# Alternating the order of the hi and lo weight products from group to group

## The chip, the cores and the metric

The kernel runs on one core of a Trainium2 chip. The metric is the device time of one execution in microseconds (us). Before the change it was 2684.91 us, the median of three runs (2683.16 to 2685.52). A profiled execution is one more run, with the hardware profiler on.

## The reference

The program is the trunk of a decoder with two layers, for 256 tokens of width 2048, in f32. Cut to what matters here:

```python
for layer in range(2):                       # 0: Mamba-2 SSD mixer, 1: RG-LRU mixer
    h = h + mixer(rms_norm(h), in_proj, ..., out_proj)
    h = h + (silu(u @ w_gate) * (u @ w_up)) @ w_down       # u = rms_norm(h), FFN of 5632
    h = h + (sigmoid(rms_norm(h) @ ple_gate)) * (p @ ple_up)
out = rms_norm(h)
# SSD: z, xbc, dt = split(u @ in_proj); short convolution, silu, chunked scan over 64 heads, gated norm
# RG-LRU: gate, xr = split(u @ in_proj); short convolution, block gates, linear scan, gelu(gate) * state
```

Nearly all the arithmetic lies in products of the activations with weights that are read once from memory in f32. (The real gate of the FFN and the per-layer embedding have their own norms; their form plays no part below.)

## The kernel before

Every weight matrix is cut into panels of 512 output columns. `panel()` computes one: it takes four PSUM banks (of eight), one for each 128 columns, and adds up the products over all blocks k of 128 input rows. The precision of f32 is kept by splitting: an activation block x holds its rounded half and the rest side by side, 128 x 512; a weight block is split into a rounded part `hi` and a rest `lo`. A weight block goes into the sum by a product of hi with all of x (128 x 512, line 268) and a product of lo with the first half of x (128 x 256, line 265).

Weights come in tiles `raw` of two k by 512 columns (512 KB, a DMA from SyncE's queue, line 231; five buffers). ScalarE casts a raw tile to a hi tile (line 239), VectorE subtracts and leaves a lo tile (line 240); each has four buffers. One tile serves eight products (two k by four banks). `group()` takes up 16 products of each kind, that is two hi tiles and two lo tiles: first 16 hi products, then 16 lo products. In the last group of a panel the second half is sorted by bank, so that bank 0 is complete first. A panel with 16 k has four groups. The last panel of the program takes its last group in another way (`apart`); the change leaves that as it was.

Behind the products, `product()` counts and now and then advances two queues of other work: `post` (what follows a panel: totals of banks, convolutions, activations, gates) and `side` (the SSD scan). These put small instructions on VectorE and ScalarE and transposes on TensorE (lines 448 and 507: transposes of sp, cs and xs in the SSD part) between the products. The total of a bank is a copy by ScalarE (line 153) and an add by VectorE (line 156). The scheduler of the language orders the instructions of every engine at build time; each engine then runs its list strictly in that order, and waits where an operand isn't there. So when the products ask for their tiles in another order, the lists of all the engines come out different.

Names that the text below uses: `a_neg`, `sp_624`, `sp_625`, `dt_v`, `adt`, `cs` belong to the step sizes and their running sums in the SSD part, in the first panels (lines 364 to 452); `sums` is a table in DRAM made from cs by DMAs (line 105), from which the tiles `e` of the scan are read; `xs` are the SSD inputs behind their activation; `gt`, `th`, `xc` belong to the RG-LRU (lines 354 to 669).

Of the kernel before, what the change touches and what calls it, by code (L numbers as in the profile page):

```python
# [18 lines left out]
T = 256  # L19
# [25 lines left out]
class Trunk:  # L45
# [197 lines left out]
    def panel(self, w, xs, pump=1.4, kt=KG, nb=NB, pre=None, post=True, apart=False):  # L243

        nc = self.nc
        banks = [self.bank() for _ in range(nb)]
        nk = w.shape[0] * kt
        todo = []
        size = RUN // nb
        count = [0, 0]

        def product(j, k, part, lo):
            b, x, wt = banks[j], xs[k], part[lo][:, j * P:(j + 1) * P]
            if apart and j == nb - 1:  # L260
                for h in range(1 if lo else 2):
                    nc.tensor.matmul(b[:, :T], wt, x[:, h * T:(h + 1) * T], start=k + lo + h == 0,
                                     stop=lo == 1 and k == nk - 1, skip_group_check=True)
            elif lo:
                self.last_product = nc.tensor.matmul(b[:, T:], wt, x[:, :T], start=False, stop=k == nk - 1,  # L265
                                                     skip_group_check=True)
            else:
                self.last_product = nc.tensor.matmul(b, wt, x, start=k == 0, stop=False, skip_group_check=True)  # L268

            count[0] += 1 if lo else 2  # L270
            while count[0] >= 3 * nb * (count[1] + 1):
                count[1] += 1
                if post:
                    self.advance(self.post)
                self.pump(pump)

        def group(last):
            if last and apart:
                for j in range(nb):
                    for lo in (0, 1):  # L280
                        for k, part in todo:
                            product(j, k, part, lo)
            else:
                for k, part in todo:
                    for j in range(nb):
                        product(j, k, part, 0)
                order = [(j, k, part) for k, part in todo for j in range(nb)]
                if last:
                    order.sort(key=lambda o: o[0])
                for j, k, part in order:  # L290
                    product(j, k, part, 1)
            todo.clear()

        k = 0
        for g in range(w.shape[0]):
            for parts in self.weights(w[g], nb * P, kt, pre and (lambda: pre(g)), bool(pre) and g < 2):
                for part in parts:
                    todo.append((k, part))
                    k += 1
                    if k == nk or len(todo) == size and not (apart and k > nk - 2 * size):  # L300
                        group(k == nk)
        if post:
            self.drain_post()
        return banks
# [579 lines left out]
```

## Time and profile before

| | |
|---|---|
| median of three runs | 2684.91 us |
| profiled execution, its own time | 2682.07 us |
| its span in the trace | 2680.3 us |
| granted TensorE clock, mean | 0.996 |
| TensorE busy | 2648.2 us (99%) |
| VectorE busy | 1822.4 us (68%) |
| ScalarE busy | 1501.7 us (56%) |
| GpSimd busy | 32.5 us (1%) |

Busy time is the time in which an engine executes. Rows of a timeline give the start, the length, the engine, the source line, the operation, output and inputs, and the number of instructions of that form in a row; in brackets stands the idle time just before, and what ended it. Matmuls overlap, so a row of products ends after the next one begins; the distance between starts is what counts.

### The profile page before, as it was taken

What the parts mean: (1) busy time and instruction counts of PE and PEld (TensorE: products, weight loads), DVE (VectorE), ACT (ScalarE), POOL (GpSimd) and SP (SyncE); (2) the same over time, 40 slices, a digit from 0 to 9 for tenths busy, and PEclk for the clock granted to TensorE, in tenths of its full rate; (3) what the DMA queues carried; (4) which work ended last, traced back from release to release, by engine and by line L of the source; (5) the groups of instructions that cost most, each with busy time, mean ns of one, the idle gap of its engine ahead of it and who ended that gap; (6) DMA issues with size and microseconds to landing.
All of it is one profiled execution on the core that took longest, in us unless ns stands there. A gap on an engine that the chain in (4) does not pass through costs nothing.

```text
span 2680.3 us, 40689 instructions
## 1 busy us (share of the span) xinstructions
PE 2648.2 (99%) x15346; PEld 2334.0 (87%) x15346; DVE 1822.4 (68%) x3066; ACT 1501.7 (56%) x2399; POOL 32.5 (1%) x70
## 2 busy tenths in 40 slices
PE   9899999999999999999999999999999999999998
PEld 7788888888888888888888888888888888888887
DVE  7888878855566655555666899977666555665667
ACT  7677755544444444444455678856444444444555
POOL 0011100000000000000000000000000000000000
PEclk9999999999999999999999999999999999999999
DMA  6767655555555555555655565555555555556553
GB/s 232 244 209 219 190 181 184 186 189 189 184 193 189 189 182 190 195 190 189 194 187 188 172 195 176 196 189 189 189 189 189 196 190 180 189 193 202 186 187 125
DMA packets 141915, 510.77 MB, mean 191 GB/s; under 512 B 15901, under 2 KB 16349, under 8 KB 141661
## 3 DMA queue, kind: packets, MB, share of 16 engines
q1 hardware_dynamic: 141719, 508.18, 57.9%
q8 instruction: 120, 1.97, 0.3%
q14 instruction: 76, 0.62, 0.1%
HBM read 505.92 MB, written 5.05 MB: 191 GB/s over the span
## 4 chain that ended last, share of the span: by engine, by line
PE 90%; DVE 6%; ACT 2%; issue 1%; DMA 1%; SPq 0%; DVEq 0%; ACTq 0%
PE bank L268 58%; PE bank L265 30%; DVE c L356 1%; DVE lo L240 1%; ACT hi L239 1%; DVE t L156 1%; DMA raw<-in_w_ssd_in_dram 1%; PE bank L523 1%; DVE t L163 1%; DVE xc L356 0%; PE bank L625 0%; ACT L88 0%; PE bank L525 0%; PE bank L507 0%; ACT s L153 0%
## 5 line engine op out<-in xcount | busy, mean ns | idle before, releaser
L268 PE MATMUL bank<-x,hi 128*128 128x512 f32 x7360 | 1771.7, 392 | 12.0 <-ACT hi L239 9.9
L268 PEld LDWEIGHTS bank<-x,hi 128*128 128x128 f32 x7360 | 1351.6, 189 | 277.4 <-ACT hi L239 12.7
L239 ACT CAST hi<-raw 128x1024 fp32r<-128x1024 f32 (+1 forms) x932 | 972.1, 1048 | 1031.6 <-PE bank L268 962.6
L240 DVE TENSOR_TENSOR lo<-raw,hi 128x1024 fp32r<-128x1024 f32 (+1 forms) x932 | 1107.2, 1220 | 503.4 <-issue 431.1
L265 PEld LDWEIGHTS bank<-x,lo 128*128 128x128 f32 x7360 | 949.5, 191 | 42.0 <-DVE lo L240 4.8
L265 PE MATMUL bank<-x,lo 128*128 128x256 f32 x7360 | 967.2, 283 | 4.4 <-DVE lo L240 4.4
L156 DVE TENSOR_TENSOR t<-bank,s 128x256 f32<-128x256 f32 x448 | 161.9, 418 | 291.3 <-ACT s L153 290.5
L153 ACT COPY s<-bank 128x256 f32<-128x256 f32 x496 | 160.3, 374 | 13.4 <-PE bank L265 4.8
L163 DVE TENSOR_TENSOR t<-t,r 128x256 f32<-128x256 f32 x216 | 83.2, 427 | 0.0
L356 DVE SCALAR_TENSOR_TENSOR c<-t,vecs,c 128x255 f32<-128x255 f32 (+1 forms) x144 | 63.1, 487 | 0.1
L145 ACT ACTIVATE x<-h,vecs 128x256 fp32r<-128x256 f32 x96 | 47.4, 501 | 17.0 <-DVE h L337 13.8
L88 ACT ACT_TABLE_LOAD x43 | 55.2, 1283 | 1.1 <-DVE c L356 0.3
L337 DVE TENSOR_TENSOR h<-h,t 128x256 f32<-128x256 f32 x144 | 54.2, 420 | 0.2
L146 DVE SCALAR_TENSOR_TENSOR x<-h,vecs,x 128x256 fp32r<-128x256 f32 x96 | 45.5, 480 | 5.9 <-ACT x L145 5.9
L88 ACT ACTIVATE e<-e,ncs 128x256 f32<-128x256 f32 (+1 forms) x128 | 45.3, 442 | 0.1
L176 DVE TENSOR_TENSOR acc<-acc,q 128x256 f32<-128x256 f32 x104 | 43.8, 421 | 2.2 <-ACT q L169 1.4
L169 ACT ACTIVATE q<-h 128x256 f32<-128x256 f32 x104 | 41.4, 405 | 4.7 <-DVE h L337 3.8
L88 ACT ACTIVATE sg<-t 128x256 f32<-128x256 f32 x88 | 32.3, 412 | 18.7 <-DVE t L163 18.7
L137 ACT CAST x<-t 128x256 fp32r<-128x256 f32 x88 | 31.8, 403 | 18.8 <-DVE t L717 18.8
L488 DVE TENSOR_TENSOR e<-e,cm 128x768 f32<-128x768 f32 x32 | 31.0, 970 | 12.6 <-ACT e L88 6.5
L403 POOL TENSOR_SCALAR_AFFINE_SELECT e<-e 128x256 f32<-128x256 f32 x64 | 31.8, 519 | 274.1 <-DMA e<-sums 236.7
L138 DVE TENSOR_TENSOR x<-t,x 128x256 fp32r<-128x256 f32 x88 | 33.3, 421 | 0.0
(121 smaller groups left out, 679.1 us busy)
## 6 DMA issues: line engine op xcount, KB each, us to landing
raw<-in_w_ffn_in_dram SPq DMA_DIRECT2D x352, 512.0 KB, 4.6
raw<-in_w_ffn_out_dram SPq DMA_DIRECT2D x176, 512.0 KB, 4.4
raw<-in_w_ssd_in_dram SPq DMA_DIRECT2D x158, 512.0 KB, 4.5
raw<-in_w_ssd_out_dram SPq DMA_DIRECT2D x64, 512.0 KB, 4.3
raw<-in_w_ple_gate_dram SPq DMA_DIRECT2D x64, 512.0 KB, 4.3
raw<-in_w_lru_in_dram SPq DMA_DIRECT2D x64, 512.0 KB, 4.2
raw<-in_w_lru_out_dram SPq DMA_DIRECT2D x32, 512.0 KB, 4.7
e<-sums SPq DMA_DIRECT2D x32, 384.0 KB, 6.0
```

The costliest lines, as they stand in the source:

```text
L88: i = self.nc.scalar.activation(out, in_, func, **kw).ins
L145: nc.scalar.activation(x[:, :T], src, AF.Copy, scale=w)
L146: nc.vector.scalar_tensor_tensor(x[:, T:], src, w, x[:, :T].bitcast(F32), ALU.mult, ALU.subtract)
L153: nc.scalar.copy(s, b[:, T:])
L156: nc.vector.tensor_tensor(t, b[:, :T], s, ALU.add)
L163: self.nc.vector.tensor_tensor(t, t, r, ALU.mult)
L239: self.last_hi = nc.scalar.copy(hi, src).ins
L240: nc.vector.tensor_tensor(lo, src, hi.bitcast(F32), ALU.subtract)
L265: self.last_product = nc.tensor.matmul(b[:, T:], wt, x[:, :T], start=False, stop=k == nk - 1, skip_group_check=True)
L268: self.last_product = nc.tensor.matmul(b, wt, x, start=k == 0, stop=False, skip_group_check=True)
L337: self.nc.vector.tensor_tensor(hb, hb, t, ALU.add)
L356: nc.vector.scalar_tensor_tensor(out[:, d:], t[:, :T - d], self.vec(cw, (3 - d) * ntap + i), out[:, d:], ALU.mult, ALU.add)
```

## The change

Within a panel, groups of odd number (the second, the fourth) take their 16 lo products first and their 16 hi products behind them; groups of even number stay hi first. So at the boundary of an odd group the kind does not change: 32 lo products stand in a row, then 32 hi products. The last group's second half is sorted by bank as before, whichever kind it is, and the flag that ends a bank's sum goes to the last product.

```diff
-        def product(j, k, part, lo):
+        turn = [0]
+
+        def product(j, k, part, lo, stop):
...
-                self.last_product = nc.tensor.matmul(b, wt, x, start=k == 0, stop=False, skip_group_check=True)
+                self.last_product = nc.tensor.matmul(b, wt, x, start=k == 0, stop=stop, skip_group_check=True)
...
         def group(last):
+            end = lambda k: last and k == nk - 1
...
-                for k, part in todo:
-                    for j in range(nb):
-                        product(j, k, part, 0)
                 order = [(j, k, part) for k, part in todo for j in range(nb)]
+                for j, k, part in order:
+                    product(j, k, part, turn[0], False)
                 if last:
                     order.sort(key=lambda o: o[0])
+                turn[0] = 1 - turn[0]
                 for j, k, part in order:
-                    product(j, k, part, 1)
+                    product(j, k, part, turn[0], end(k))
```

The number of instructions stays the same on every engine that computes. Lines of helpers stand three lines lower in the changed file; the hi product is line 270 there, the lo product line 267. In TensorE's list a hi product is followed by a lo product 467 times before and 245 times now, a lo product by a hi product 439 times before and 245 times now.

Three places show how the lists change. First the start of the program, in the panels whose results feed the scan. TensorE before (the transposes of sp_625 and cs are line 448):

```order
L265 MATMUL bank<-x,lo 128x256 x16
L268 MATMUL bank<-x,hi 128x512 x16
L265 MATMUL bank<-x,lo 128x256 x16
L268 MATMUL bank<-x,hi 128x512 x9
L448 MATMUL bank<-ident,sp_625 128x128 x2
L268 MATMUL bank<-x,hi 128x512 x7
L265 MATMUL bank<-x,lo 128x256 x8
L448 MATMUL bank<-ident,cs 128x128 x2
```

And TensorE there now:

```order
L270 MATMUL bank<-x,hi 128x512 x32
L267 MATMUL bank<-x,lo 128x256 x32
L270 MATMUL bank<-x,hi 128x512 x3
L451 MATMUL bank<-ident,sp_625 128x128 x2
L270 MATMUL bank<-x,hi 128x512 x5
L451 MATMUL bank<-ident,cs 128x128
L270 MATMUL bank<-x,hi 128x512
L451 MATMUL bank<-ident,cs 128x128
L270 MATMUL bank<-x,hi 128x512 x23
```

The transposes of sp_625 moved from the tenth place of the next group's hi products to the fourth place of this group's, those of cs from that group's lo products to behind this group's eighth hi product.

VectorE at the same place, around the small instruction on a_neg, before:

```order
L435 TENSOR_SCALAR a_neg<-a_neg 128x1
L163 TENSOR_TENSOR t<-t,r 128x256
L370 TENSOR_TENSOR sp_623<-sp_623,sp_622 128x256
L356 SCALAR_TENSOR_TENSOR c<-t,vecs,c 128x255
L371 TENSOR_TENSOR sp_624<-sp_623 128x256
L356 SCALAR_TENSOR_TENSOR c<-t,vecs,c 128x254
```

VectorE there now:

```order
L163 TENSOR_TENSOR t<-t,r 128x256
L373 TENSOR_TENSOR sp_623<-sp_623,sp_622 128x256
L438 TENSOR_SCALAR a_neg<-a_neg 128x1
L240 TENSOR_TENSOR lo<-raw,hi 128x1024
L374 TENSOR_TENSOR sp_624<-sp_623 128x256
L359 SCALAR_TENSOR_TENSOR c<-t,vecs,c 128x255
```

The group's first lo tile moved from behind the work on c and sp_625 to directly behind a_neg; its second lo tile still follows that work.

Second, SyncE's queue a little later, where the table sums is made. Before:

```order
L231 DMA raw_1046<-in_w_ssd_in_dram 128x1024
L231 DMA raw_1052<-in_w_ssd_in_dram 128x1024
L105 DMA sums_97<-cs_692 64x384
L231 DMA raw_1104<-in_w_ssd_in_dram 128x1024
L231 DMA raw_1110<-in_w_ssd_in_dram 128x1024
L105 DMA sums_97<-sums_97 8x2x12288 x3
L105 DMA sums_97<-sums_97 5x2x12288
```

Now:

```order
L231 DMA raw_1046<-in_w_ssd_in_dram 128x1024
L105 DMA sums_97<-cs_700 64x384
L105 DMA sums_97<-sums_97 8x2x12288 x3
L105 DMA sums_97<-sums_97 5x2x12288
L231 DMA raw_1052<-in_w_ssd_in_dram 128x1024
L231 DMA raw_1104<-in_w_ssd_in_dram 128x1024
L231 DMA raw_1110<-in_w_ssd_in_dram 128x1024
```

Three weight loads moved behind all the DMAs of sums.

Third, ScalarE in the RG-LRU, around the gelu of gt. Before, with the names of the weight tiles:

```order
L239 CAST hi_16834<-raw_16832 128x1024
L88 ACT_TABLE_LOAD
L88 ACTIVATE th0_16652<-th0_16652 128x256 x2
L88 ACTIVATE th1_16653<-th1_16653 128x256 x2
L88 ACT_TABLE_LOAD
L88 ACTIVATE gt0_16148<-gt0_16148 128x256 x2
L88 ACTIVATE gt1_16149<-gt1_16149 128x256 x2
```

Now:

```order
L88 ACT_TABLE_LOAD
L88 ACTIVATE gt0_16148<-gt0_16148 128x256 x2
L88 ACTIVATE gt1_16149<-gt1_16149 128x256 x2
L153 COPY s_16810<-bank_16514 128x256
L153 COPY s_16814<-bank_16515 128x256
L153 COPY s_16818<-bank_16516 128x256
L239 CAST hi_16834<-raw_16832 128x1024
```

The cast of the tile from raw_16832 moved from ahead of both table loads to behind the gelu and three copies.

## Rows read from the trace of the kernel before

**Rows 1.** The page, busy time, share of the span and instructions of each engine

```profile
PE 2648.2 (99%) x15346; PEld 2334.0 (87%) x15346; DVE 1822.4 (68%) x3066; ACT 1501.7 (56%) x2399; POOL 32.5 (1%) x70
```

**Rows 2.** The page's costliest groups: busy, mean ns, idle time before and what ended it

```profile
L268 PE MATMUL bank<-x,hi 128*128 128x512 f32 x7360 | 1771.7, 392 | 12.0 <-ACT hi L239 9.9
L265 PE MATMUL bank<-x,lo 128*128 128x256 f32 x7360 | 967.2, 283 | 4.4 <-DVE lo L240 4.4
```

**Rows 3.** Timeline of TensorE in the program's last panel: start, length, line, operation

```profile
2654.24 2.00 PE L268 MATMUL bank<-x,hi 128*128 128x512 f32 x8
...
2662.62 0.64 PE L262 MATMUL bank<-x,hi 128*128 128x256 f32 x4
```

**Rows 4.** Timeline of TensorE in panels of the RG-LRU's output

```profile
1800.43 3.82 PE L268 MATMUL bank<-x,hi 128*128 128x512 f32 x16
...
1839.39 3.82 PE L268 MATMUL bank<-x,hi 128*128 128x512 f32 x16
```

**Rows 5.** Timeline of TensorE around the transposes of xs, third head group

```profile
206.38 0.49 PE L507 MATMUL bank<-ident,xs 128*128 128x128 f32 x3
207.22 0.33 PE L507 MATMUL bank<-ident,xs 128*128 128x128 f32 x1 [0.35 <-ACT xs L88]
207.30 3.00 PE L268 MATMUL bank<-x,hi 128*128 128x512 f32 x12
210.14 0.60 PE L507 MATMUL bank<-ident,xs 128*128 128x128 f32 x4
210.50 0.71 PE L268 MATMUL bank<-x,hi 128*128 128x512 f32 x2
```

**Rows 6.** Line 507, idle time of its queues until: us, times

```profile
  ACT xs L88: 6.0, 11
```

**Rows 7.** Timeline of TensorE at the program's start

```profile
64.45 3.82 PE L268 MATMUL bank<-x,hi 128*128 128x512 f32 x16
72.67 3.78 PE L265 MATMUL bank<-x,lo 128*128 128x256 f32 x16 [4.39 <-DVE lo L240]
76.24 2.64 PE L268 MATMUL bank<-x,hi 128*128 128x512 f32 x9
```

**Rows 8.** Stretch of TensorE: length, busy (products), granted clock, DMA share, GB/s

```profile
72.60:76.20 3.60, 3.54 (x16) 0.50 0.69 175
```

**Rows 9.** Timeline of VectorE in the same stretch

```profile
65.75 0.15 DVE L435 TENSOR_SCALAR a_neg<-a_neg 128x1 f32<-128x1 f32 x1 [0.95 <-ACT a_neg L88]
...
66.48 0.48 DVE L356 SCALAR_TENSOR_TENSOR c<-t,vecs,c 128x255 f32<-128x255 f32 x1
...
71.39 1.22 DVE L240 TENSOR_TENSOR lo<-raw,hi 128x1024 fp32r<-128x1024 f32 x1
...
76.67 0.42 DVE L380 TENSOR_TENSOR sp<-sp,sp 128x256 f32<-128x256 f32 x1
```

**Rows 10.** Timeline of ScalarE, a cast behind a weight load

```profile
76.20 1.05 ACT L239 CAST hi<-raw 128x1024 fp32r<-128x1024 f32 x1 [2.47 <-DMA raw<-in_w_ssd_in_dram]
```

**Rows 11.** Timeline of SyncE's DMA issues

```profile
84.54 2.86 SPq L105 DMA_DIRECT2D sums<-sums  x4
87.93 4.32 SPq L231 DMA_DIRECT2D raw<-in_w_ssd_in_dram  x2
```

**Rows 12.** Timeline of ScalarE, the cast of the first of these two loads

```profile
104.60 1.05 ACT L239 CAST hi<-raw 128x1024 fp32r<-128x1024 f32 x1 [4.34 <-DMA raw<-in_w_ssd_in_dram]
```

**Rows 13.** Timeline of ScalarE in the RG-LRU

```profile
1634.74 1.34 ACT L88 ACTIVATE gt<-gt 128x256 f32<-128x256 f32 x4
1635.98 0.90 ACT L153 COPY s<-bank 128x256 f32<-128x256 f32 x3
```

**Rows 14.** Timeline of TensorE in the RG-LRU

```profile
1636.03 3.96 PE L268 MATMUL bank<-x,hi 128*128 128x512 f32 x16
```

**Rows 15.** Timeline of VectorE behind an output panel

```profile
1420.83 2.35 DVE L240 TENSOR_TENSOR lo<-raw,hi 128x1024 fp32r<-128x1024 f32 x2
```

**Rows 16.** Timeline of TensorE there

```profile
1421.89 3.82 PE L268 MATMUL bank<-x,hi 128*128 128x512 f32 x16
```

## What the change is expected to do: the prediction

> **What bounds the kernel now.** I read the page's shares first. TensorE is busy for 2648.2 of 2680.3 us, VectorE and ScalarE much less [rows 1], so only what makes TensorE shorter, or makes it wait, counts. In the costliest groups the reader is to see the idle time in front of the products: 12.0 us before the hi products, 4.4 us before the lo products, over 7360 of each [rows 2]. The hi and lo tiles are thus nearly always there in time, and the question is whether they still are when another kind is asked for first. Then come the timelines: the spacing of starts tells what a switch of kind costs, and at four places the rows of VectorE, ScalarE and SyncE tell when a tile is made and when it would now be wanted.
>
> The sum is made against the profiled execution's own 2682.07 us, 1.8 us around its span of 2680.3; it lies 2.84 us under the median, 2684.91, so 2.84 is added at the end. A change under 0.2%, 5.4 us, counts here as no change: from 2679.5 to 2690.3.
>
> **Switches removed.** The last panel takes 8 hi and 8 lo products in turn: three periods from 2654.24 to 2662.62 [rows 3], 2.793 us each, so 16 + 16 products with two pairs of switches take 5.587. In groups of 16 + 16 seven periods run from 1800.43 to 1839.39 [rows 4], 5.566 each, with one pair. A pair of switches costs 0.021 us. By the counts in the section on the change, 222 switches from hi to lo and 194 from lo to hi go, 208 pairs: **-4.2 us**. No gain of another kind is in the products: their number and shapes stay, and both rows are full streams.
>
> The Trainium skill, in "TensorE: Matmul & The Clock Gate", section "Back-to-back issue gap", gives the distance of products that are taken singly as their columns at 2.4 GHz and 2.5 ns more, whatever stood before. By it regrouping is worth nothing, and the sum would be 4.2 us higher. The trace has a difference, though one of 0.02 us in 5.6.
>
> **Transposes of xs in the SSD part.** Behind the panels of a head group, four transposes wait for the last xs on ScalarE. The first four take from 206.38 to the next product at 207.30, 0.92 us with a wait of 0.35; the second four, with nothing to wait for, from 210.14 to 210.50, 0.36 [rows 5]. So 0.56 us per head group where it occurs; the line's queues waited 11 times, 6.0 us [rows 6], and that counts TensorE and its weight loads both, about five head groups. In the new order ScalarE makes xs earlier against the products, and the lo tiles wanted in its place are made in time by VectorE, so I take the whole: 5 x 0.56 = **-2.8 us** (from 0 to -3.0, half of the 6.0).
>
> **The program's start.** This is the largest loss. Before, the hi products of one group begin at 64.45, then TensorE waits 4.39 us for the first lo tile, the lo products begin at 72.67, and the next group's hi products at 76.24 [rows 7]. The 16 lo products in 72.60 to 76.20 run at half the clock: the granted clock there is 0.50, the level of 1.2 GHz, after the 4.39 us of idle time [rows 8].
>
> Now the lo products come first. The first lo tile stands directly behind a_neg, which ends at 65.90 [rows 9], and takes 1.22: it is there at 67.1, and eight products run. The second is still behind the work on c and sp that before filled 66.48 to 71.39 [rows 9], 4.9 us: 67.1 + 4.9 + 1.2 = 73.2. TensorE waits about five microseconds, and I assume the half clock after it for as long as before: 8 lo in 1.8 to 75.0, four hi in 1.8, twelve more at 0.23 (3.82 over 16, rows overlap, [rows 7]) in 2.7, end at 79.6 against 76.24, **+3.4**. Between these hi products now stand the transposes of sp and cs. That of sp is covered: sp was written at 76.67 to 77.09 [rows 9], now a little earlier, and TensorE is there at about 76.4. cs is not: VectorE makes it behind a lo tile whose hi cast, held by its load, ends at 77.25 [rows 10]; add 1.2 for that lo tile and about 1.4 for the scans (four small instructions, the size of those in [rows 9]), so 79.8, and TensorE is there at 78.2: **+1.6**. Together +5.0.
>
> Then SyncE: three weight loads now stand behind the DMAs of sums. The first two loads that stood behind them before were issued from 87.93, and sums from 84.54 [rows 11], and the first was there only at 104.60, when its cast began after 4.34 us of waiting [rows 12]: 16.7 us from issue to use. Now sums is issued some two microseconds earlier, since cs has fewer lo tiles before it on VectorE, and the first load behind it at about 85.7. By the same 16.7 it would be cast at 102.4 and its lo tile ready at 104.7 (1.05 and 1.22). It is wanted by the fourth group after this one, lo first, second tile: 76.24 + 5.0 + three groups of 5.566 + 0.6 for the transposes, about 98.5, and 0.96 for the first tile's eight products: 99.5. The loss is between 0, if the load overtakes the copies, and 5.2 and another 1.7 for the clock (16 products at half of it took 3.57, from 72.67 to 76.24, in place of 1.91). I take 2, nearer to nothing, since in the rows of before the queue also carried two loads ahead of sums. The start: **+7 us**, from +3.4 to +11.9.
>
> **RG-LRU.** ScalarE cast the first hi tile of the group at 1636.03 [rows 14] ahead of both table loads. Now it stands behind gt (1634.74 + 1.34) and three copies that end at 1636.8 [rows 13]: ready at 1637.8, **+1.8** (0 if the list before it has become shorter). The lo tiles of the next, lo first, group are wanted 3.65 us earlier, and VectorE has seven instructions of some 0.48 ahead of the second one, up to 3.4; later tiles of this stretch would be late too, but a wait there gives the others time. I take +2.2: **+4.0 us** in all, from 0 to +5.2.
>
> **Output panels.** Where totals and norms lie ahead of the lo tiles on VectorE, the order of these does not change. Two lo tiles take 1420.83 to 1423.18 [rows 15]; a group that begins at 1421.89 [rows 16] lo first wants the first at once and the second 0.96 later. The first is ready at 1422.05 (+0.16), the second at 1423.18 against 1423.01 (+0.17): 0.33 us. I count 14 such panels, from FFN, SSD and RG-LRU outputs: **+4.6 us** (from 0, if the totals too come earlier, since the sorted half is now the longer one). In the FFN's input panels, more than half of all groups, VectorE has time, and I cost the earlier lo tiles at nothing; if that cover were gone, each group would lose what the output panels lose.
>
> **The sum.** -4.2 - 2.8 + 7 + 4.0 + 4.6 = +8.6. 2682.07 + 8.6 + 2.84 = **2693.5 us**.
>
> **Rivals.** 1. *The new lists hide every loss* (faster). The scheduler knows when a lo tile is wanted and may have put each in time; the gain in switches and xs stays: -7.0, 2677.9 us. For it: idle time ahead of products is only 16 us now [rows 2], so tiles have time. Against it: the first lo tile moved, the second did not. 0.16.
>
> 2. *Only the start's own wait remains* (no change). The load behind sums overtakes it, and the RG-LRU and output panels absorb their lateness: -7.0 + 5.0 = -2.0, 2682.9 us. For it: the waits of a few tenths in the output panels are within the error of such a count. Against it: the order of ScalarE at gt. 0.24.
>
> 3. *A switch costs nothing*, the rest as forecast: 2697.7 us. Against it stand rows 3 and 4; for it that they differ by 0.02 us only, near the hundredth in which they are given. 0.08. This is what the Trainium skill's rule in "Back-to-back issue gap" would make of it.
>
> 4. *The loads behind sums hold up the start in full*, and the half clock follows: start +11.9, RG-LRU +5.2, outputs +4.6, gains -7.0: +14.7, 2699.6 us. For it: the one load that the rows show behind sums took 16.7 us. 0.15.
>
> **How the numbers follow.** The forecast has 0.37. It and rivals 1 to 4 make 1. The forecast's own range is 2688 to 2699; a seventh of it falls within no change. So faster 0.16, no change 0.24 + 0.05 = 0.29, slower 0.55. The range for 8 in 10 leaves out the lower half of rival 1 and the far end of rival 4: 2678 to 2703.
>
> **What would show it.** In the changed kernel's timeline of TensorE: a wait for a lo tile between eight and eight lo products near 68 to 73, a wait at the transposes of cs near 78 to 80, and one for a lo or hi tile near 99 to 105; waits for hi near 1636; idle time of tenths ahead of lo products behind output panels. In the page, line 267's idle time would rise from 4.4 to about 15 us, and the transposes' waits for xs vanish. It is wrong if switches turn out to be worth clearly more than 0.02 us a pair, if idle time ahead of lo products does not rise, or if SyncE's loads behind sums land within a few microseconds of their issue.

## The result, and the profile after

The changed kernel takes 2707.28 us (median of four runs, 2707.11 to 2707.64), the kernel before, in the same session, 2685.22. The ratio is 1.0083, 95% interval 1.0065 to 1.0100: 22 us slower. The forecast was slower, 2693.5 us, in a range up to 2703; the direction was right, but the forecast change, 8.6 us, is less than half of the measured one.

The page after, first the busy times, then the groups of the two products (columns as in [rows 2]):

```profile
span 2705.6 us, 40570 instructions
PE 2656.3 (98%) x15346; PEld 2342.8 (87%) x15346; DVE 1866.9 (69%) x3066; ACT 1502.5 (56%) x2399; POOL 42.9 (2%) x70
...
L270 PE MATMUL bank<-x,hi 128*128 128x512 f32 x7360 | 1737.7, 392 | 6.7 <-ACT hi L239 6.0
...
L267 PE MATMUL bank<-x,lo 128*128 128x256 f32 x7360 | 944.1, 285 | 29.9 <-DVE lo L240 29.6
```

Against [rows 1, 2] the reader is to see two things. The wait ahead of the lo products rose from 4.4 to 29.9 us, as the new order asks for lo first. And TensorE is busy 8.1 us longer (2648.2 to 2656.3) with the same products: some ran at the lower clock. (The two groups' own busy times fell, because the overlap of a hi with a lo product at a switch counts in both, and there are fewer switches.) The span grew by 25.3; what isn't busy, 17.2 us, is waiting. The profiled execution of the kernel before lies 3 us under its median, so differences between the traces are 3 us larger than the 22 of the medians.

Where the time goes is best seen from the start of the weight product that has n others before it in both traces (the RG-LRU's small gate products left out), and their difference. Products 0 to 2592 are the SSD's input panels, the first head panel from 544, the last eight panels, for the gate z, from 1568; its output panels end at 3616, the first FFN at 7904, the first embedding at 8416, the RG-LRU at 9952.

| product | start before | later after by |
|---|---|---|
| 128 | 30.4 | 3.1 |
| 384 | 82.7 | 6.5 |
| 512 | 105.7 | 13.8 |
| 640 | 129.4 | 17.9 |
| 704 | 146.3 | 15.3 |
| 1664 | 351.9 | 11.6 |
| 7680 | 1405.2 | 10.2 |
| 8704 | 1589.6 | 11.7 |
| 9216 | 1693.3 | 25.2 |
| 14080 | 2547.7 | 24.5 |
| last | 2665.4 | 25.4 |

The start costs 15.3 us: 3.1 in the first panel, 3.4 up to product 384, 7.4 up to 512, 1.4 up to 704. (The 17.9 at product 640 sets a product behind a wait against one that in the kernel before has its wait still ahead.) The SSD's head groups give 3.7 back, the panels up to 7680 a little more, and the RG-LRU costs 13.5.

**The start.** TensorE's timeline after, in the stretch of [rows 7], and, ahead of it, two waits in the first panel:

```profile
13.35 1.22 PE L267 MATMUL bank<-x,lo 128*128 128x256 f32 x8 [0.32 <-DVE lo L240]
16.08 2.08 PE L267 MATMUL bank<-x,lo 128*128 128x256 f32 x8 [1.51 <-DVE lo L240]
...
69.92 1.45 PE L267 MATMUL bank<-x,lo 128*128 128x256 f32 x8 [2.22 <-DVE lo L240]
76.30 2.08 PE L267 MATMUL bank<-x,lo 128*128 128x256 f32 x8 [4.93 <-DVE lo L240]
78.18 1.48 PE L270 MATMUL bank<-x,hi 128*128 128x512 f32 x3
79.46 0.63 PE L451 MATMUL bank<-ident,sp 128*128 128x128 f32 x2
79.74 1.96 PE L270 MATMUL bank<-x,hi 128*128 128x512 f32 x5
81.54 0.27 PE L451 MATMUL bank<-ident,cs 128*128 128x128 f32 x1
```

VectorE there, the rows that answer to [rows 9]:

```profile
68.58 0.15 DVE L438 TENSOR_SCALAR a_neg<-a_neg 128x1 f32<-128x1 f32 x1 [0.35 <-ACT a_neg L88]
68.65 1.22 DVE L240 TENSOR_TENSOR lo<-raw,hi 128x1024 fp32r<-128x1024 f32 x1
...
75.03 1.22 DVE L240 TENSOR_TENSOR lo<-raw,hi 128x1024 fp32r<-128x1024 f32 x1
```

The two lo tiles start 6.4 us apart, the second behind the work on c and sp, and TensorE waits 4.93 us between eight and eight lo products. The transposes of sp and cs (line 451) wait for nothing.

Next come two waits that the table shows at products 512 and 640. SyncE's issues, the cast of the first load behind sums, and TensorE:

```profile
85.64 2.86 SPq L105 DMA_DIRECT2D sums<-sums  x4
88.60 10.09 SPq L231 DMA_DIRECT2D raw<-in_w_ssd_in_dram  x5
```

```profile
104.90 1.04 ACT L239 CAST hi<-raw 128x1024 fp32r<-128x1024 f32 x1 [1.96 <-DMA raw<-in_w_ssd_in_dram]
...
144.80 3.88 ACT L239 CAST hi<-raw 128x1024 fp32r<-128x1024 f32 x4
```

```profile
107.25 2.07 PE L267 MATMUL bank<-x,lo 128*128 128x256 f32 x8 [5.87 <-DVE lo L240]
...
147.31 2.93 PE L267 MATMUL bank<-x,lo 128*128 128x256 f32 x12 [4.69 <-DVE lo L240]
```

The load issued at 88.60 is cast at 104.90, 16.3 us later; in the kernel before it was 16.7 [rows 11, 12]. The wait at 147.31 is of another kind: the four casts at 144.80 stand in ScalarE's list behind the exponentials of the first head group. The kernel before waits at the same place, for its hi tiles:

```profile
133.57 3.87 ACT L239 CAST hi<-raw 128x1024 fp32r<-128x1024 f32 x4
...
134.65 3.38 PE L268 MATMUL bank<-x,hi 128*128 128x512 f32 x8 [3.25 <-ACT hi L239]
```

So this wait is not new; lo first, TensorE waits there for a subtraction behind the cast too, and the net loss is 1.4 us (13.8 late at product 512, 15.3 at 704).

After these waits the products run slowly. Stretches of TensorE, columns as in [rows 8] (length, busy, granted clock):

```profile
16.00:20.00 4.00, 3.92 (x14) 0.57 1.04 412
...
76.00:80.00 4.00, 3.70 (x14) 0.50 0.51 136
107.20:111.00 3.80, 3.75 (x13) 0.50 0.80 256
147.00:151.00 4.00, 3.69 (x17) 0.50 0.63 181
1662.00:1666.00 4.00, 3.40 (x12) 0.50 0.51 151
```

0.50 is the level of 1.2 GHz. The kernel before has the stretch of [rows 8] and one more, behind its wait at 134.65.

**RG-LRU.** Three of TensorE's waits, and VectorE at the second of these:

```profile
1604.28 1.22 PE L267 MATMUL bank<-x,lo 128*128 128x256 f32 x8 [1.49 <-DVE lo L240]
...
1662.61 1.65 PE L267 MATMUL bank<-x,lo 128*128 128x256 f32 x6 [2.44 <-DVE lo L240]
...
1706.03 2.08 PE L267 MATMUL bank<-x,lo 128*128 128x256 f32 x8 [2.35 <-DVE lo L240]
```

```profile
1657.67 1.22 DVE L240 TENSOR_TENSOR lo<-raw,hi 128x1024 fp32r<-128x1024 f32 x1
1658.81 0.42 DVE L138 TENSOR_TENSOR x<-xc,x 128x256 fp32r<-128x256 f32 x1
1659.14 0.42 DVE L138 TENSOR_TENSOR x<-gt,x 128x256 fp32r<-128x256 f32 x1
...
1661.33 1.22 DVE L240 TENSOR_TENSOR lo<-raw,hi 128x1024 fp32r<-128x1024 f32 x1
```

Between the two tiles stand seven small instructions, VectorE is never idle, and TensorE waits 2.44 us. In all there are six waits for lo tiles in the RG-LRU, 9.6 us, and one for a hi tile, 0.56 us.

### The profile page after: what moved, and what is told of

It is laid out like the page before. It is cut to its first block, busy times and chain, and to the rows that moved or that the text cites. A ratio compares the mean times of both kernels' runs of the same rounds, so it can differ in the third digit from the quotient of the medians.

```text
span 2705.6 us, 40570 instructions
## 1 busy us (share of the span) xinstructions
PE 2656.3 (98%) x15346; PEld 2342.8 (87%) x15346; DVE 1866.9 (69%) x3066; ACT 1502.5 (56%) x2399; POOL 42.9 (2%) x70
## 4 chain that ended last, share of the span: by engine, by line
PE 89%; issue 6%; DVE 4%; ACT 1%; POOL 0%; DVEq 0%; POOLq 0%; ACTq 0%
PE bank L270 57%; PE bank L267 30%; DVE lo L240 1%; PE bank L526 1%; PE bank L628 0%; DVE t L156 0%; ACT hi L239 0%; DVE h L340 0%; DVE acc L176 0%; PE bank L528 0%; PE bank L510 0%; PE bank L630 0%; POOL e L406 0%; PE bank L187 0%; DVE xc L359 0%
## 5 line engine op out<-in xcount | busy, mean ns | idle before, releaser
L270 PE MATMUL bank<-x,hi 128*128 128x512 f32 x7360 | 1737.7, 392 | 6.7 <-ACT hi L239 6.0
L270 PEld LDWEIGHTS bank<-x,hi 128*128 128x128 f32 x7360 | 1367.4, 189 | 281.6 <-ACT hi L239 7.2
L240 DVE TENSOR_TENSOR lo<-raw,hi 128x1024 fp32r<-128x1024 f32 (+1 forms) x932 | 1119.3, 1221 | 589.1 <-ACT hi L239 368.3
L267 PEld LDWEIGHTS bank<-x,lo 128*128 128x128 f32 x7360 | 926.1, 192 | 56.5 <-DVE lo L240 34.2
L267 PE MATMUL bank<-x,lo 128*128 128x256 f32 x7360 | 944.1, 285 | 29.9 <-DVE lo L240 29.6
L153 ACT COPY s<-bank 128x256 f32<-128x256 f32 x496 | 178.5, 371 | 389.0 <-PE bank L270 373.9
L156 DVE TENSOR_TENSOR t<-bank,s 128x256 f32<-128x256 f32 x448 | 184.8, 421 | 167.6 <-ACT s L153 164.8
L359 DVE SCALAR_TENSOR_TENSOR c<-t,vecs,c 128x255 f32<-128x255 f32 (+2 forms) x144 | 65.5, 498 | 0.5 <-ACT c L357 0.4
L491 DVE TENSOR_TENSOR e<-e,cm 128x768 f32<-128x768 f32 x32 | 31.0, 968 | 19.4 <-issue 10.4
L720 DVE TENSOR_TENSOR t<-t,sg 128x256 f32<-128x256 f32 x88 | 37.2, 422 | 1.5
L714 DVE TENSOR_TENSOR sg<-sg,r 128x256 f32<-128x256 f32 x88 | 34.8, 420 | 0.7
```

The source lines that it names most:

```text
L153: nc.scalar.copy(s, b[:, T:])
L156: nc.vector.tensor_tensor(t, b[:, :T], s, ALU.add)
L240: nc.vector.tensor_tensor(lo, src, hi.bitcast(F32), ALU.subtract)
L359: nc.vector.scalar_tensor_tensor(out[:, d:], t[:, :T - d], self.vec(cw, (3 - d) * ntap + i), out[:, d:], ALU.mult, ALU.add)
```

## The experiments

Theory A: the loss is made at single places where a tile stands late in VectorE's or ScalarE's list or behind sums in the queue, made larger by the lower clock behind the wait. Theory B: every alternated group costs a little. Theory C: buffers and loads, not lists, make the tiles late. A list is the order of one engine's instructions. Ratios are to the kernel before, run on the same chip beside each set (medians 2682.9 to 2683.1).

**Parts of the program.** A flag chooses per panel whether the order alternates:

```diff
                 for j, k, part in order:
                     product(j, k, part, turn[0], end(k))
+                turn[0] = turn[0] if self.swap else 0
```

Only in the six first panels. Expected:

> Alternating only in the six first panels (the four B, C panels, dt, and the first head panel). Theory A, the loss is made at single places, where a lo tile asked for early stands late in VectorE's list, and the idle time there puts the TensorE clock to its lower level for some microseconds: the start alone costs +13 to +18 us on before, since the changed kernel is 17.9 us late after the sixth panel, and later waits for xs give a part back or not. Theory B, every alternated group costs a little, the same everywhere: six of about 120 panels cost no more than 2 us.

Measured: 2695.39 us, +12.4; ratio 1.0047 (1.0033 to 1.0061). That is a little under the range expected. (The profiled execution took 2698.20; in its trace the kernel is 15.9 us late at product 704 and 16.8 at 1664.)

Only in the RG-LRU's input panels and first four output panels. Expected:

> Alternating only in the RG-LRU's input panels and its first four output panels. Theory A: the changed kernel goes from 11.7 to 25.2 us late in this stretch, so alone it costs +11 to +14 us. Theory B (the same small cost in all groups): 12 of about 120 panels, +2 to +3 us.

Measured: 2699.77 us, +16.7; 1.0062 (1.0048 to 1.0076). That is above the range expected: in the trace 3.2 us are lost in the RG-LRU's first input panel, where the changed kernel loses nothing.

Everywhere else. Expected:

> Alternating everywhere but in these two stretches: the SSD's other panels, output panels, FFN, per-layer embedding. Theory A: what remains is the gain, -0.02 us for a pair of switches, some 180 pairs, and the waits for xs in the SSD part if these panels make them go: -4 to -7 us against before. Theory B: the loss stays, +15 to +20 us.

Measured: 2683.49 us, +0.4; 1.0001 (0.9992 to 1.0010).

Theory B falls: nearly the whole loss is in the first two parts. The gain expected of the rest did not come. Its trace has the waits for xs gone, but three small ones for lo in the head groups, between 160 and 360 us, in their place (us, times, longest):

```profile
PE bank L268 <- DVE lo L241: 1.0, 3, 0.4
```

At product 704 it is 1.5 us late, in panels that are unchanged (the kernel with the RG-LRU's order alone is 1.4 late there); the difference is 1.0 at product 5120, 0.6 at 7680, and 1.5 at the end, since the panels around the embedding take back what switches give. The three parts add up to +29.5 against +22.1. Two reasons can be seen in the traces: the head groups gave 3.7 us back only where they alternate behind a late start (0.9 lost with the start's order alone, 0.4 with the rest's), and the RG-LRU alone lost 3.2 in its first panel.

**Loads ahead of sums.** Six more steps of the side work ahead of the DMAs of sums:

```diff
             self.dts, self.ncs = dts, ncs
             yield
             yield
+            for _ in range(6):
+                yield
```

> The changed kernel with the DMAs of sums six steps later in the side work, so that the load of raw_1048 and the two behind it are issued ahead of most of sums, as before. If the wait of 5.87 us near 101 is the load behind the sums copies, it goes and with it the half clock behind it: -5 to -8 us against the changed kernel (+14 to +17 on before), unless tiles e come later and the first head group waits for them. If that wait comes from the order on VectorE or ScalarE alone, the time stays within 1 us of the changed kernel's +22.

Measured: 2698.59 us, ratio 1.0059 (1.0043 to 1.0074), +15.5, so 6.5 below the changed kernel, as expected. One load now goes ahead of the copies within sums, two between them:

```profile
88.00 0.33 SPq L231 DMA_DIRECT2D raw<-in_w_ssd_in_dram  x1
88.38 1.46 SPq L105 DMA_DIRECT2D sums<-sums  x2
89.94 1.05 SPq L231 DMA_DIRECT2D raw<-in_w_ssd_in_dram  x2
91.04 1.41 SPq L105 DMA_DIRECT2D sums<-sums  x2
```

TensorE at that place:

```profile
102.77 7.44 PE L270 MATMUL bank<-x,hi 128*128 128x512 f32 x32
110.05 2.07 PE L267 MATMUL bank<-x,lo 128*128 128x256 f32 x16
113.28 2.43 PE L267 MATMUL bank<-x,lo 128*128 128x256 f32 x16 [1.16 <-DVE lo L240]
```

The wait of 5.87 is gone; at product 512 the kernel is 7.6 us late, not 13.8. The load behind sums cost 6.2 us, wait and slow products together. Behind that place the two kernels differ in other ways too (5.2 against 15.3 us late at product 800, 4.9 against 11.6 at 1664), so that the 6.5 of the totals is not this wait alone.

**The place in the list.** The scheduler takes a priority for what it is given; here hi and lo tiles get one some instructions earlier, in the RG-LRU panels alone:

```diff
+            with self.tc.high_priority(self.lead):
                 self.last_hi = nc.scalar.copy(hi, src).ins
                 nc.vector.tensor_tensor(lo, src, hi.bitcast(F32), ALU.subtract)
```

> The changed kernel; only in the RG-LRU's input panels and first four output panels the casts and subtractions that make hi and lo tiles get a priority 80 instructions earlier in the scheduler, so they stand ahead of gates, scans and convolutions in ScalarE's and VectorE's lists. Products and buffers stay. Theory A (lo tiles are late by their place in VectorE's list): the waits for lo between 1595 and 1710 go, and the half clock behind them: the stretch costs some 0 to 5 us in place of 13.5, so -8 to -13 us against the changed kernel, +9 to +14 on before. Theory C (tiles are late because their four buffers come free too late, or their loads land too late): no list can help, the time stays at +22 on before within 2 us.

Measured: 2697.9 us, +15.0; 1.0054 (1.0039 to 1.0069), 7 below the changed kernel, 1 short of the range expected. Waits between 1590 and 1710, changed kernel and this one (us, times, longest):

```profile
PE bank L267 <- DVE lo L240: 9.6, 6, 2.4
PE bank L270 <- ACT hi L239: 0.6, 1, 0.6
```

```profile
PE bank L269 <- DVE lo L242: 3.1, 4, 0.9
PE bank L272 <- DVE t L157: 1.2, 1, 1.2
...
```

Products and buffers are the same, and most of the wait went; the stretch from product 8704 to 9216 costs 5.9 us, not 13.5. Theory C falls for the RG-LRU: most of its loss is one of lists. It did not go wholly: waits for lo of 3.1 us remain, and one for t, the total of a bank, is new.

The same in all panels, by 80 and by 160 instructions, and in the kernel before:

> The changed kernel with that priority in all panels. Theory A: the losses at the start shrink too, where they come from lists (first lo tiles, the five microseconds near 71, the load behind sums, since sums moves in SyncE's queue): -10 to -20 us against the changed kernel, +2 to +12 on before; side work that now comes later may cost some of it. Theory C: at the start loads and buffers decide, and no more than 3 us are won there.

> As before, 160 instructions earlier. Theory A: as with 80, or a little better in the RG-LRU; if side work becomes late, totals hold up banks and the time is longer than with 80 by some microseconds. Theory C: no difference to the changed kernel.

> The kernel before with the same priority of 80, as a control: if the priority is worth something of itself (the waits of 9.9 and 4.4 us for hi and lo tiles in before), -2 to -8 us; if only the new order needs it, within 2 us of before.

Measured: 2711.73 (1.0107, 1.0090 to 1.0124), 2718.29 (1.0129, 1.0114 to 1.0144) and 2712.40 us (1.0108, 1.0092 to 1.0123). All three expectations missed in the total; only the guess that 160 might take some microseconds longer than 80 came true. The traces say why. At product 1664 the changed kernel with 80 is 1.1 us late and with 160 1.6 us early, against 11.6 without: the whole loss of the start, against the kernel before, can be taken away by lists. In the RG-LRU 80 lowers the loss to 4.4 us, but 160 leaves 11.8: waits for t have taken the place of those for lo. And 13 to 15 us are lost in each of two other places, the same in the kernel before, where a short panel of the per-layer embedding has its totals (up) behind the tiles that got the priority. The kernel before with 80:

```profile
PE bank L269 <- DVE up L156: 18.1, 4, 4.7
```

**A version made of the pieces.** The changed order except in the RG-LRU's input and first four output panels; priority 160 in the SSD's input panels only; in a second version also 80 in output panels and most of the FFN; as a control, the kernel before with 160 in the SSD's input panels:

```diff
+        self.lead = 160
...
+        self.lead = 0
         self.out_product(w_out, yn, "norm_ffn", 0)
...
+            self.swap = int(kind == "o" and n >= 4)
             if kind == "x":
```

> The changed order everywhere but in the RG-LRU's input panels and first four output panels; hi and lo tiles get a priority 160 instructions earlier in the SSD's input panels only. If the losses are local, the pieces add up from the traces: -1.5 us after the SSD part (the changed kernel with that priority), -0.02 us for each pair of switches in the FFN and the embedding, some 1 us lost at output panels: -2 to -4 us against before. That would be below what can be told from no change, so a verdict of slower by more than 3 us would speak against the sum.

> The same, with a priority of 80 also in the output panels and the FFN's, but not in the last FFN output group nor in the embedding, where the runs before lost 13 us each. In these runs the loss of 1 us behind output panels was gone, so -3 to -5 us against before; if the priority delays totals there, slower by several us in the FFN.

> The kernel before with a priority of 160 in the SSD's input panels only, and no change of order: a control. If the gain of the mixed kernels in that part comes from the priority, it is here too, -1 to -3 us after the SSD part in the trace. If the order is needed for it, 0 to +3.

Measured: 2679.35 us, 0.9985 (0.9976 to 0.9994), -3.7; 2679.91, 0.9984 (0.9975 to 0.9992); control 2681.71, 0.9995 (0.9986 to 1.0004). Both versions beat the kernel before by an interval clear of 1, by little; the second adds nothing to the first. The control's interval against the kernel before overlaps theirs, but set side by side all eleven runs of the first version (2678.17 to 2680.35) lie below all ten of the control (2680.80 to 2684.46): 2.4 us between the medians go with the changed order. The traces show where. The control is 5.4 us early at product 1664, more than the first version (2.9), so the gain at the start is the priority's and does not need the order. By product 2592 the control has lost 5.1 of it again, some 0.7 in each of seven panels, where among other things its transposes of rs_y now wait 0.2; the first version loses nothing there and gains 1.7 more up to product 7360, the size of its fewer switches. TensorE of the first version at the start:

```profile
63.91 4.00 PE L270 MATMUL bank<-x,lo 128*128 128x256 f32 x32
67.74 7.44 PE L273 MATMUL bank<-x,hi 128*128 128x512 f32 x32
75.02 4.00 PE L270 MATMUL bank<-x,lo 128*128 128x256 f32 x32
...
107.60 2.08 PE L270 MATMUL bank<-x,lo 128*128 128x256 f32 x8 [5.51 <-DVE lo L243]
```

The waits of this stretch, 4.39 us in [rows 7] and 7.15 in the changed kernel, are both gone. The wait at 107.60, for a load behind sums, is still there; the version was not run with sums later.

**The price of a switch.** Groups of 8 and 8 in the kernel before (RUN = 8 in place of 16):

> The kernel before with groups of 8 hi and 8 lo products in place of 16 and 16: switches from hi to lo rise from 529 to 987, from lo to hi from 507 to 956, some 450 pairs more. By 0.02 us a pair the stretches of the FFN without waits get longer by 0.06 us in each 16.7 (three groups), +9 us in all; if a switch costs nothing, those stretches keep their length. Lo tiles are wanted 1.8 us earlier than before, so at the start and in the RG-LRU some waits as in the changed kernel may appear, smaller ones.

Measured: 2703.12 us, +20.1; 1.0071 (1.0057 to 1.0085). In the FFN, where there are no waits, six periods of 8 + 8 run from the first row to the last:

```profile
1000.91 2.00 PE L268 MATMUL bank<-x,hi 128*128 128x512 f32 x8
...
1017.67 0.63 PE L268 MATMUL bank<-x,hi 128*128 128x512 f32 x2
```

That is 2.793 us a period, 5.587 for two, as in the last panel [rows 3], against 5.566 [rows 4]. Over 2176 products without a wait (3000 to 5176) this kernel loses 1.37 us, 68 pairs more, 0.020 each; the changed kernel wins 0.66 there, 34 pairs fewer, 0.019 each. So a pair has its price. The Trainium skill, in "TensorE: Matmul & The Clock Gate", section "Back-to-back issue gap", gives the distance of products taken singly from their columns alone; by it the pair would be free (rival 3). These three kernels do not agree with it, and the measurement decides. At that price some 9 of the 20 us are the switches'. What the expectation didn't foresee lies around the short panels of the embedding (6.2 us between products 7168 and 7680, 7.7 between 13568 and 14080), with waits for up again. At the start and in the RG-LRU, where it expected waits, this kernel gains 2.5 us up to product 1664 and loses 0.6 from 8704 to 9216.

## Why the prediction was half right

Between the two traces lie 25.3 us, 16.7 more than the sum's 8.6. Of these, 8.3 lie in the start and 9.5 in the RG-LRU; the other terms together came out 1.1 lower than forecast.

**Switches, -4.2.** Right: 0.019 to 0.020 us a pair in two kernels. Idle-free stretches gain 0.4 us in 1280 products.

**Transposes of xs, -2.8.** Right in the changed kernel: line 510 has no wait for xs at all, and the head groups gave 3.7 us from product 704 to 1664, some 0.3 of it switches. But it hung on a condition that the prediction did not have: where the start is not late, small waits for lo take its place.

**The program's start, +7.** This step failed in size: +15.3 at product 704, outside the term's own end of +11.9. Of its parts, the second lo tile behind c and sp was right: 4.93 us of waiting, about five foreseen, half clock behind it, and 3.4 us lost up to product 384 beside the first panel's 3.1, as forecast. The later group's wait behind sums was foreseen too, but not its price: taken at 2 us, 6.2 by the experiment, near the upper end that had been worked out from the one row that showed a load behind sums [rows 11, 12]. That row should have decided: 16.7 us then, 16.3 now, without the two loads ahead of sums that were the reason for the low price. The wait for cs, 1.6, did not come. Two losses were not foreseen: 1.8 us of waiting in the first panel, before 20 us, with a slow stretch behind it, 3.1 in all; and 1.4 us net at the wait of 147.31, which in the kernel before was one of 3.25 us for a hi tile. The prediction priced two groups of the start and passed by the others, before and behind them.

**RG-LRU, +4.0.** Failed in size: +13.5 (products 8704 to 9216), outside 0 to +5.2. At the place that was priced, the mechanism for lo was right: seven instructions ahead of the second lo tile, a wait of 2.44 us, 2.2 foreseen; the priority run shows that lists cause most of the loss. The hi tile behind gelu, priced at 1.8, cost 0.56. The step that failed is the sentence that later tiles would be late too but a wait there gives the others time. VectorE had been busy for 95.07 of the 100 us from 1590 to 1690 in the kernel before, and the waits repeat: six of them, 9.6 us, three ahead of the group that was priced and one behind it, and where the clock fell behind them the products of 1662 to 1666 ran at half of it.

**Output panels, +4.6.** Too high: 1.2 us between products 7680 and 8320 and 0.9 from 14080 to the end, net of switches, so in the FFN's last output panels and in the embedding. Beyond the gain in switches nothing changes at the SSD's output panels (11.4 late at product 2592, 11.1 at 3616) or at the first half of the FFN's (10.6 at 5152, 10.4 at 5920). One panel's rows were carried to 14.

**The clock.** The forecast charged it at one wait, and only the upper end of the start at a second. In the trace TensorE was busy for 27.0 us at the level of 1.2 GHz, against 7.8 before (the program's last microseconds left out). By an estimate, half of the difference, 9.6 us, would have been saved at the full clock: nearly two fifths of the 25.3. In the first panel 1.8 us of waiting cost 3.1.

Rival 4, everything at its upper end, 2699.6, came nearest. Rival 1 lost in the changed kernel; the version made of pieces shows lists in which most of the start's losses are hidden, with the RG-LRU left in the old order.

## What to carry to other kernels

When products are reordered, ask of every reordered group when its last tile is made, not only of those where a wait is seen now; where an engine that makes tiles is full, expect lateness to repeat rather than to be absorbed. Price a wait with the slow products behind it if the trace shows one such pair anywhere. A priority for the tiles cures what lists cause, but only stage by stage: given everywhere it lost 13 us and more in each of two places that had waited 0.4 us before.

## What the runs showed of the hardware

A pair of switches between products of 512 and of 256 columns costs 0.02 us. A load issued 3.0 to 3.4 us after the first of four copies within DRAM was used 16 to 17 us later, in both traces, where the loads of this matrix land in a median of 4.5 us before and 4.3 after. In the run with sums later, the load ahead of the copies landed 3.5 us after its issue (88.00 to 91.53), the first behind two of them 10.9 (89.94 to 100.83), the first behind all four 18.0 (92.89 to 110.85). After the wait of 1.51 us at 16.08 the granted clock was 0.57 in the next 4 us; after that of 1.49 us at 1604.28 it stayed: 1.00 in 1598 to 1620. So the length of a single wait does not tell whether the clock falls.
